# Two rows of their own for a token's two expert products, and scatters that skip empty slots

## The chip, the core and the metric

The kernel runs on one core of one Trainium2 chip. Time is device microseconds of one execution of the whole program. TensorE (PE) does the matmuls, VectorE (DVE), ScalarE (ACT) and GpSimd (POOL) the rest, SyncE (SP) issues loads. DMAs issued from SP and ACT and the indirect DMAs (a list of row numbers on chip says which rows of DRAM are read or written) issued from POOL move the data.

## The reference

Two layers of a diffusion network over 512 tokens of width 1024 (256 latent, 256 context). Layer 0 is neighbourhood attention and an mLSTM, then a mixture of experts; layer 1 is grouped-query attention, then a mixture of experts over the latent tokens. What is touched is the mixture of layer 0:

```python
def moe(h, router_w, router_b, w1, w3, w2):
    ...                                  # sigmoid scores, the best group of 4 experts,
    _, local = lax.top_k(sel_in, TOP_K)  # its two best experts
    e_idx = g_idx[:, None] * EXP_PER_GROUP + local
    w = jnp.take_along_axis(scores, e_idx, axis=-1)
    w = w / w.sum(axis=-1, keepdims=True)
    ...
    for e in range(N_EXPERTS):
        y = y + comb[:, e:e + 1] * ((jax.nn.silu(h @ w1[e]) * (h @ w3[e])) @ w2[e])
```

16 experts, 512 tokens, two experts for each: 1,024 products of a token and an expert, each a row of 1024 numbers, and each token's result is the sum of its two.

## The kernel before

Everything is float32. Weights come in pieces of 1 MB (`wtile`, L132, `w`) by SP into a ring of slots; for most matmuls each piece is split by ACT (`hi`, L286) and DVE (`lo`, L287) into two halves of the precision, and PE does three products instead of one.

**The first expert stage** (`moe_rows`, L509 onwards) lies at about 412 to 660 us. The router gives each product a place in a list of its expert (`pos`) and a weight (`wts`). Products are worked in 12 blocks of 128 slots: nine blocks hold one expert, three ("small", blocks 2, 5, 8, 11) hold two experts of 64 slots each. Experts 0 and 1 are fixed as blocks 0 and 1; the others are sorted by their counts into places (`lpos`, `lwts`). So 1,536 slots take 1,024 products. For block i:

- `table(i)` (L632) makes, from a one-hot matrix `oh` and matmuls into a PSUM tile `ad`, the list of row numbers `idx` (L612), the weights `we` (L613) and, in small blocks, a second list `idx2` (L640) for the upper 64 slots. Each list has six buffers. An empty slot gets the number 512 + slot (`home`, `pcol`). It then issues on POOL `gather` (L625): 128 rows of `rows` in DRAM go to `xg`. `table(i)` is written four blocks ahead of its use (`LEAD`).
- `x_turn`, `up`, `gated`, `a_turn`, `down_` transpose the rows and do the two projections up, the product, and the projection down.
- In `down_` the rows are multiplied with `we` into `ys`, and `scatter` (L630) adds them into `yacc` in DRAM, by an indirect DMA that accumulates. Small blocks do this in two halves of 64 rows, one made by ACT (L759) and one by DVE (L760). Blocks 10 and 11 (`DIR`) are not scattered; matmuls put them back on chip at the end (`put_back`, L909).

At the end, `yacc` is read back by two DMAs of 1 MB (L889) into slots of the weight ring, added to `put_back`'s sums by matmuls with an identity (`sums`, L915), and the residual is formed on DVE (`residual0`, L774).

**The clearing.** Adding needs zeros: `clear` (L1569) fills with zeros the rows 512 to 639 of `rows` and all 640 rows of `yacc`, by six DMAs of 512 KB on ACT's queue. It is called in the middle of layer 0's attention, about 218 to 229 us. Near it stand attention's exponentials on ACT (L1466) and the copies of projected values `mo` out of the PSUM tile `pj` (L1562); PE transposes into `pj` (L208) and runs the projection L1358 between pieces of attention.

**What sets the order.** Instructions stand on each engine in the order that a scheduler gives them at build time from the order of the code and its own estimates of durations; each engine runs its list in order. A buffer that is used again makes its writer wait for the last reader. Each DMA of SP and ACT signals one of eight semaphores (DMAHW0 to 7) in turn, and waits until the last DMA on its semaphore has landed; POOL's do the same with eight others (DMASW0 to 7).

Of the kernel before, what the change touches and what calls it, by code (L numbers as in the profile page):

```python
# [16 lines left out]
P = 128  # L17
# [66 lines left out]
def _model(tc, nc, ctx, A, out, dbg):  # L84
# [80 lines left out]
    for b in range(NB):  # L165
        V.tensor_scalar(pcol[:, b:b + 1], pidx, float(b * P - T), None, op0=OP.add)
    home = const.tile([P, 1], F32, name="home")
    V.tensor_scalar(home, pidx, float(T), None, op0=OP.add)
    sl = const.tile([P, J, 32], F32, name="sl")
# [155 lines left out]
    def moe_front(l, lat0, A2, pool):  # L325
# [36 lines left out]
        def finish(rt, put_row, brow, lgb, counts=None):  # L362
# [63 lines left out]
            rows_half(1)  # L426
            return pos, wts, msk

# [90 lines left out]
    def moe_rows(finish, shift, rows, yacc, fst, st, rt, ahead1, stream):  # L519
# [24 lines left out]

        pos, wts, msk = finish(rt, put_row, *shift, counts)
        bg(99)
# [9 lines left out]
        lpos, lwts = rt.tile([P, nb, NE], F32, name="lpos"), rt.tile([P, nb, NE], F32, name="lwts")  # L556
        GP.memset(aux[:, :, :, 3].bitcast(F32), 0.0)

# [64 lines left out]
        def gather(idx, tag="xg"):  # L623
            xg = wt_([P, D], tag)
            GP.indirect_dma_start(out=xg, out_offset=None, in_=rows[:, :],  # L625
                                  in_offset=bass.IndirectOffsetOnAxis(ap=idx[:, :1], axis=0))
            return xg

        def scatter(ys, idx):
            GP.indirect_dma_start(out=yacc[:, :], out_offset=bass.IndirectOffsetOnAxis(ap=idx[:, :1], axis=0),  # L630
                                  in_=ys, in_offset=None, compute_op=OP.add)

        def table(i):
            l, m = BLOCKS[i][0], len(BLOCKS[i])
            IDX[i], WE[i] = wt_([P, 1], "idx", I32), wt_([P, 1], "we")
            oh = one_hot(i)
            tb = slot_rows(oh, lambda b: aux[:, b, l:l + m, :], IDX[i], WE[i], m)
            if m == 2:
                IDX2[i] = wt_([HALF, 1], "idx2", I32)
                V.tensor_tensor(IDX2[i], tb[HALF:, 4:5], home[HALF:], op=OP.add)  # L640
            if i:
                XG[i] = gather(IDX[i])
            return oh
# [86 lines left out]
        def down_(i):  # L730
# [18 lines left out]
            if i in DIR:  # L749
                Y[i] = wt_([P, D], "ys" if i < DIR[-1] else "xh", F32R), wt_([P, D], "xg", F32R)  # L750
                for c in range(2):
                    yh, yl = (y[:, c * 512:(c + 1) * 512] for y in Y[i])
                    SC.activation(yh, yp[c], AF.Copy, scale=WE[i])
                    V.scalar_tensor_tensor(yl, yp[c], WE[i], yh.bitcast(F32), op0=OP.mult, op1=OP.subtract)
            elif is_small(i):
                ys = [wt_([P, D], "ys")[0:HALF] for _ in range(2)]
                for c in range(2):
                    s = slice(c * 512, (c + 1) * 512)
                    SC.activation(ys[0][:, s], yp[c][0:HALF], AF.Copy, scale=WE[i][0:HALF])  # L759
                    V.tensor_tensor(ys[1][:, s], yp[c][HALF:], WE[i][HALF:, 0:1].to_broadcast([HALF, 512]), op=OP.mult)  # L760

                scatter(ys[0], IDX[i][0:HALF])
                scatter(ys[1], IDX2[i])
            else:
                ys = wt_([P, D], "ys")
                for c in range(2):
                    SC.activation(ys[:, c * 512:(c + 1) * 512], yp[c], AF.Copy, scale=WE[i])
                scatter(ys, IDX[i])
            yield
# [18 lines left out]

        for dst, src in ((lpos, pos), (lwts, wts)):
            for b in range(0, nb, 2):  # L790
# [71 lines left out]
        with tc.issue_after(turned0.ins):  # L862
            put_aux(aux[:, :, FIX:], lpos[:, :, FIX:], lwts[:, :, FIX:])

# [8 lines left out]
        for i in range(n_ + 1):  # L873
# [9 lines left out]
            if i == n_:  # L883
                while stream.todo:
                    stream.load()
                ahead1(AH1)
                yr = [wslot().rearrange("p (a c) -> p a c", a=2) for _ in range(2)]
                for b in range(2):
                    pin(SY.dma_start(yr[b], yacc[b * 2 * P:(b + 1) * 2 * P, :].rearrange("(a p) c -> p a c", p=P)))  # L889
                ahead1(6)  # L890
# [41 lines left out]
    def moe_chip(finish, shift, fst, rt, rowp):  # L932
# [20 lines left out]

        pos, wts, msk = finish(rt, put_row, *shift, counts)
        fst.close()
# [609 lines left out]

    rows = dram.tile([T + P, D], F32, name="rows")
    yacc = dram.tile([T + P, D], F32, name="yacc")

    def clear(dep):  # L1569

        V.tensor_scalar(jp, ones, dep, 0.0, op0=OP.mult, op1=OP.mult)
        z = jp[:, None, :].to_broadcast([P, J, P])
        SC.dma_start(rows[T:, :].rearrange("p (a c) -> p a c", a=J), z)
        for b in range(NB + 1):
            SC.dma_start(yacc[b * P:(b + 1) * P, :].rearrange("p (a c) -> p a c", a=J), z)
# [452 lines left out]
```

## Time and profile before

| | |
|---|---|
| time, three runs | 1099.27, 1099.69, 1100.06 us (median 1099.69) |
| profiled execution | 1100.19 us, span 1098.3 us |
| mean granted TensorE clock | 0.958 of full speed |
| PE busy | 984.2 us (90% of the span) |
| DVE, ACT, POOL busy | 559.7, 399.6, 91.1 us |
| weight queue q1 | 290.23 MB, 66.8% of the span of 16 DMA engines |
| gathers and scatters, q0 | 11.01 MB, 3.8% |
| queue q10, with the clearing | 3.47 MB, 1.1% |
| indirect DMAs of the first expert stage | 11 gathers, 13 scatters |

The span runs from the first instruction to the last, and the time includes what lies around it. The share of busy time is a mean over stages with different limits, so the rows further down are of single stretches. A DMA share of 1 says that all 16 DMA engines had work the whole time. "Idle before, <- X" says for how long the engine had stood still ahead of an instruction, and what it waited for last.

### The profile page before, as it was taken

How to read it: one execution, taken by the hardware profiler on the slowest of the kernel's cores; microseconds unless marked ns; L12 is line 12 of the kernel's file. 1: busy time of each engine (PE TensorE's matmuls, PEld its weight loads, DVE VectorE, ACT ScalarE, POOL GpSimd, SP SyncE). 2: the span in 40 equal slices, each digit the busy share in tenths (PEclk: the TensorE clock that was granted, in tenths of full speed). 3: DMA queues.
4: the chain of work that ended last, by engine and by line, in shares of the span. 5: the costliest groups of instructions: out<-in, count | busy, mean ns of one | idle time of the engine just before them, and what ended most of it. 6: DMA issues, size and time to landing. Idle time of an engine off the chain costs nothing.

```text
span 1098.3 us, 14558 instructions
## 1 busy us (share of the span) xinstructions
PE 984.2 (90%) x5327; PEld 616.7 (56%) x5327; DVE 559.7 (51%) x1333; ACT 399.6 (36%) x735; POOL 91.1 (8%) x87
## 2 busy tenths in 40 slices
PE   5799999999999559999899999799998899988865
PEld 1577845556776357565566545468766454433322
DVE  3543389645877659575465623745766621101101
ACT  2532254437445227464535533324344121111100
POOL 0300000002000301211120100410100100000000
PEclk9899999999999769999989999899999799999988
DMA  9932237492328519999999999560198599999993
GB/s 376 300 123 83 77 146 256 168 340 77 123 109 322 215 56 361 388 392 395 401 404 383 409 401 371 201 232 2 61 357 348 205 419 420 420 419 420 421 419 113
DMA packets 71580, 305.70 MB, mean 278 GB/s; under 512 B 6096, under 2 KB 27856, under 8 KB 41168
## 3 DMA queue, kind: packets, MB, share of 16 engines
q1 hardware_dynamic: 61904, 290.23, 66.8%
q0 software_dynamic: 3072, 11.01, 3.8%
q10 hardware_dynamic: 6528, 3.47, 1.1%
q8 instruction: 44, 0.72, 0.3%
q14 instruction: 32, 0.26, 0.1%
HBM read 293.16 MB, written 11.53 MB: 277 GB/s over the span
## 4 chain that ended last, share of the span: by engine, by line
PE 30%; DMA 14%; DVE 4%; ACT 1%; issue 1%; POOL 0%; SPq 0%; DVEq 0%; ACTq 0%; POOLq 0%
DMA w<-in_exp_w_dram 13%; PE o L1011 5%; PE pj L1358 4%; PE o L235 3%; PE o L1050 2%; PE o L1886 1%; PE t L1358 1%; PE pj L998 1%; PE a L1871 1%; PE a L261 1%; PE o L1358 1%; DVE lo L287 1%; DMA xg<-rows,idx 1%; PE ad L261 1%; PE t L1882 1%; PE t L681 1%
## 5 line engine op out<-in xcount | busy, mean ns | idle before, releaser
L287 DVE TENSOR_TENSOR lo<-w,hi 128x1024 fp32r<-128x1024 f32 (+2 forms) x170 | 179.6, 1077 | 52.2 <-ACT hi L286 45.7
L286 ACT CAST hi<-w 128x1024 fp32r<-128x1024 f32 (+2 forms) x172 | 156.7, 928 | 111.0 <-PE o L1358 37.8
L1011 PE MATMUL o<-w,x 128*64 128x512 f32 x280 | 67.8, 596 | 0.0
L1028 DVE TENSOR_TENSOR ac<-ac,o 64x512 f32<-64x512 f32 x13 | 9.0, 691 | 110.5 <-ACT ac L1027 110.5
L702 PE MATMUL o<-lo,xh 128*128 128x512 f32 x128 | 51.8, 404 | 6.8 <-DVE lo L287 6.8
L681 PE MATMUL o<-w,xh 128*64 128x512 f32 x128 | 56.2, 595 | 0.1
L683 PE MATMUL o<-w,xh 128*64 128x512 f32 x128 | 56.2, 594 | 0.0
L261 PE MATMUL ad<-w,sl 128*32 128x512 f32 x320 | 50.8, 614 | 3.2 <-DMA w<-in_ada_w_dram 3.1
L701 PE MATMUL o<-hi,xh 128*128 128x512 f32 x128 | 51.6, 403 | 2.2 <-ACT hi L286 1.7
L703 PE MATMUL o<-hi,xl 128*128 128x512 f32 x128 | 50.9, 398 | 0.9 <-DVE xl L652 0.9
L1358 PE MATMUL pj<-h_hi,hi 128*128 128x512 f32 x104 | 43.8, 421 | 5.0 <-ACT h_hi L1345 2.6
L1027 ACT ACTIVATE ac<-o 64x512 f32<-64x512 f32 x13 | 7.7, 590 | 107.9 <-PE o L1011 63.2
L1358 PE MATMUL pj<-h_hi,lo 128*128 128x512 f32 x104 | 43.4, 418 | 0.2 <-DVE lo L287 0.2
L1358 PE MATMUL pj<-h_lo,hi 128*128 128x512 f32 x104 | 43.4, 417 | 0.0
L1011 PEld LDWEIGHTS o<-w,x 128*64 128x64 f32 x280 | 20.6, 137 | 37.9 <-issue 36.6
L235 PE MATMUL o<-w,x 128*32 128x512 f32 x256 | 31.4, 637 | 7.6 <-DMA w<-in_exp_w_dram 7.6
L681 PEld LDWEIGHTS o<-w,xh 128*64 128x64 f32 x128 | 17.0, 137 | 34.6 <-issue 33.4
L710 DVE TENSOR_TENSOR ac<-ac,o 128x512 f32<-128x512 f32 x12 | 8.2, 684 | 49.7 <-PE o L683 46.1
L1050 PE MATMUL o<-w,at 128*64 128x512 f32 x120 | 33.0, 597 | 0.0
L702 PEld LDWEIGHTS o<-lo,xh 128*128 128x128 f32 x128 | 24.6, 192 | 14.5 <-DVE lo L287 9.7
L1081 DVE SCALAR_TENSOR_TENSOR yl<-o,we,yh 128x512 fp32r<-128x512 f32 x12 | 8.9, 750 | 40.9 <-ACT yh L1080 40.9
L701 PEld LDWEIGHTS o<-hi,xh 128*128 128x128 f32 x128 | 24.5, 191 | 9.3 <-ACT hi L286 3.5
(589 smaller groups left out, 2269.4 us busy)
## 6 DMA issues: line engine op xcount, KB each, us to landing
w<-in_exp_w_dram SPq DMA_DIRECT2D x190, 1024.0 KB, 18.4
w<-in_ada_w_dram SPq DMA_DIRECT2D x48, 1024.0 KB, 6.7
w<-in_even_w_in_dram SPq DMA_DIRECT2D x12, 1024.0 KB, 12.1
w<-in_odd_w_in_dram SPq DMA_DIRECT2D x6, 1024.0 KB, 12.6
XT<-in_xT_dram SPq DMA_DIRECT2D x2, 2048.0 KB, 8.3
w<-in_even_w_out_dram SPq DMA_DIRECT2D x4, 1024.0 KB, 7.8
w<-in_odd_w_out_dram SPq DMA_DIRECT2D x4, 1024.0 KB, 9.0
yacc<-jp ACTq DMA_DIRECT2D x5, 512.0 KB, 9.7
```

The source lines that it names most:

```text
L235: done = PE.matmul(out[32 * q:32 * q + 32, :], lhsT=lhsT, rhs=rhs, start=start, stop=stop)
L261: PE.matmul(ps[32 * q:32 * q + 32, :], lhsT=sl[:, k, :], rhs=w[:, 0, q * 512:(q + 1) * 512], start=(k == 0), stop=(k == J - 1))
L286: SC.copy(hi, w)
L287: eng.tensor_tensor(lo, w, hi.bitcast(F32), op=OP.subtract)
L681: with_last = PE.matmul(out[HALF:], lhsT=lhsT[:, HALF:], rhs=rhs[1], start=start, stop=stop)
L683: PE.matmul(out[0:HALF], lhsT=lhsT[:, 0:HALF], rhs=rhs[0], start=start, stop=stop)
L701: PE.matmul(h_, lhsT=XH[i][:, k, :], rhs=hi[:, k % 2, :], start=(k == 0), stop=False)
L702: PE.matmul(h_, lhsT=XH[i][:, k, :], rhs=lo[:, k % 2, :], start=False, stop=False)
L703: PE.matmul(h_, lhsT=XL[i][:, k, :], rhs=hi[:, k % 2, :], start=False, stop=(k == J - 1))
L1011: PE.matmul(h[64 * c:64 * c + 64, :], lhsT=x[:, k, :], rhs=ws[c][:, i, :], start=(k == 0), stop=(k == J - 1))
L1050: PE.matmul(y[c][64 * i:64 * i + 64, :], lhsT=a[:, k, :], rhs=row_of(ws[q, i], k % 2)[:, c * 512:(c + 1) * 512], start=(k == 0), stop=(k = ...
L1358: f = (lambda a, b, **k: PE.matmul(ps, lhsT=b, rhs=a, **k)) if flip else (lambda a, b, **k: PE.matmul(ps, lhsT=a, rhs=b, **k))
```

## The change

In words: every token has two rows in `yacc`, row t for its first and row 512 + t for its second product, so that no two products meet and nothing has to be added in DRAM. The router's rank of a product among its token's two (0 or 1, `rank`) travels with `pos` (coded as rank * 1024 + pos through the sorting, decoded behind it) into the fourth column of `aux`, and from there into `idx2`, which every scattered block now has. Scatters are plain writes; an empty slot's number is 1,024 or more, and a bounds check skips it, in gathers too. A small block makes one `ys` of 128 rows (both halves by ACT) and one scatter: ten scatters instead of 13. `yacc` has 1,024 rows: eight clearing DMAs of 512 KB instead of five, and none for `rows` any more, so eight in place of six. Four reads of 1 MB bring `yacc` back, and four additions on DVE join the second half to the first ahead of `sums`.

```diff
-        V.tensor_scalar(pcol[:, b:b + 1], pidx, float(b * P - T), None, op0=OP.add)
+        V.tensor_scalar(pcol[:, b:b + 1], pidx, float(b * P - 2 * T), None, op0=OP.add)
...
-    V.tensor_scalar(home, pidx, float(T), None, op0=OP.add)
+    V.tensor_scalar(home, pidx, float(2 * T), None, op0=OP.add)
...
         put_aux(aux[:, :, 0:FIX], pos[:, :, 0:FIX], wts[:, :, 0:FIX])
+        V.tensor_scalar(aux[:, :, 0:FIX, 3], turn_[:, :, 0:FIX], float(T), None, op0=OP.mult)
...
             GP.indirect_dma_start(out=xg, out_offset=None, in_=rows[:, :],
-                                  in_offset=bass.IndirectOffsetOnAxis(ap=idx[:, :1], axis=0))
+                                  in_offset=bass.IndirectOffsetOnAxis(ap=idx[:, :1], axis=0), bounds_check=T - 1, oob_is_err=False)
...
             GP.indirect_dma_start(out=yacc[:, :], out_offset=bass.IndirectOffsetOnAxis(ap=idx[:, :1], axis=0),
-                                  in_=ys, in_offset=None, compute_op=OP.add)
+                                  in_=ys, in_offset=None, bounds_check=2 * T - 1, oob_is_err=False)
...
-            if m == 2:
-                IDX2[i] = wt_([HALF, 1], "idx2", I32)
-                V.tensor_tensor(IDX2[i], tb[HALF:, 4:5], home[HALF:], op=OP.add)
+            if i not in DIR:
+                IDX2[i] = wt_([P, 1], "idx2", I32)
+                for k in range(m):
+                    s = slice(P // m * k, P // m * (k + 1))
+                    V.tensor_tensor(IDX2[i][s], tb[s, 4 * k + 3:4 * k + 4], IDX[i][s], op=OP.add)
...
-            elif is_small(i):
-                ys = [wt_([P, D], "ys")[0:HALF] for _ in range(2)]
...
-                    SC.activation(ys[0][:, s], yp[c][0:HALF], AF.Copy, scale=WE[i][0:HALF])
-                    V.tensor_tensor(ys[1][:, s], yp[c][HALF:], WE[i][HALF:, 0:1].to_broadcast([HALF, 512]), op=OP.mult)
-
-                scatter(ys[0], IDX[i][0:HALF])
-                scatter(ys[1], IDX2[i])
             else:
...
-                scatter(ys, IDX[i])
+                scatter(ys, IDX2[i])
...
+        V.scalar_tensor_tensor(code, turn_, 1024.0, pos, op0=OP.mult, op1=OP.add)
+        for dst, src in ((lpos, code), (lwts, wts)):
...
+            V.tensor_scalar(second, lp, 1024.0, float(T), op0=OP.is_ge, op1=OP.mult)
+            V.scalar_tensor_tensor(lp, second.bitcast(F32), -1024.0 / T, lp, op0=OP.mult, op1=OP.add)
...
-                yr = [wslot().rearrange("p (a c) -> p a c", a=2) for _ in range(2)]
-                for b in range(2):
+                yr = [wslot().rearrange("p (a c) -> p a c", a=2) for _ in range(4)]
+                for b in (0, 2, 1, 3):
                     pin(SY.dma_start(yr[b], yacc[b * 2 * P:(b + 1) * 2 * P, :].rearrange("(a p) c -> p a c", p=P)))
...
+        for b in range(2):
+            for a in range(2):
+                V.tensor_tensor(yr[b][:, a], yr[b][:, a], yr[2 + b][:, a], op=OP.add)
...
-        SC.dma_start(rows[T:, :].rearrange("p (a c) -> p a c", a=J), z)
-        for b in range(NB + 1):
+        for b in range(2 * NB):
             SC.dma_start(yacc[b * P:(b + 1) * P, :].rearrange("p (a c) -> p a c", a=J), z)
```

Three places where the order of instructions moves. First, DVE in the middle of the expert stage, where the table of block 11 is made (`idx_4964` of before and `idx_5014` of after are its list, in two halves; `idx_4776` that of block 10; `oh` a one-hot matrix, `al` and `ys` belong to earlier blocks). Before:

```order
L612 TENSOR_SCALAR idx_4776<-ad_4780,home_88 128x1 [waits DMASW7_49,DMASW4_49,PE_49]
L613 TENSOR_REDUCE we_4777<-ad_4780 128x1
L601 TENSOR_TENSOR oh_5535<-slots_75,lpos_3301 128x512
L726 TENSOR_TENSOR al_4761<-pj_4755,ah_4760 128x512 [waits Activation_49]
L601 TENSOR_TENSOR oh_5543<-slots_75,lpos_3301 128x512 [waits PE_49]
L612 TENSOR_SCALAR idx_4964<-ad_4968,home_88 64x1 [waits DMASW0_49,DVE_49]
L612 TENSOR_SCALAR idx_4964<-ad_4968,home_88 64x1
L760 TENSOR_TENSOR ys_4769<-t_4730,we_3917 64x512 [waits DMASW3_49,Activation_49]
L287 TENSOR_TENSOR lo_4803<-w_4800,hi_4802 128x1024 [waits DMAHW2_49,Activation_49]
L760 TENSOR_TENSOR ys_4769<-t_4731,we_3917 64x512 [waits Activation_49]
```

After:

```order
L612 TENSOR_SCALAR idx_4822<-ad_4826,home_88 128x1 [waits PE_49]
L613 TENSOR_REDUCE we_4823<-ad_4826 128x1
L601 TENSOR_TENSOR oh_5587<-slots_75,lpos_3303 128x512
L728 TENSOR_TENSOR al_4809<-pj_4803,ah_4808 128x512 [waits Activation_49]
L612 TENSOR_SCALAR idx_5014<-ad_5018,home_88 64x1 [waits DMASW6_49,PE_49]
L612 TENSOR_SCALAR idx_5014<-ad_5018,home_88 64x1
L601 TENSOR_TENSOR oh_5595<-slots_75,lpos_3303 128x512
L287 TENSOR_TENSOR lo_4851<-w_4848,hi_4850 128x1024 [waits DMAHW4_49,Activation_49]
L613 TENSOR_REDUCE we_5015<-ad_5018 64x1 [waits Activation_49]
```

The list of block 11 waited for DMASW0, the semaphore on which the gather of block 10 signals; now it waits for DMASW6, that of the gather of block 5 (and for PE's `ad`). The two products `ys` of a small block on DVE are gone.

Second, ACT in attention, where the clearing stands (`pT`, `oa` and `p` belong to attention). Before:

```order
L1573 DMA rows<-jp 1024x1x128 [waits DMAHW3_49]
L1575 DMA yacc<-jp 1024x1x128 [waits DMAHW4_49]
L1475 COPY pT<-t 128x4x128 [waits PE_49]
L1575 DMA yacc<-jp 1024x1x128 [waits DMAHW6_49]
L1575 DMA yacc<-jp 1024x1x128 [waits DMAHW7_49]
L1486 CAST oa<-o 128x256 [waits PE_49]
L1575 DMA yacc<-jp 1024x1x128 [waits DMAHW1_49]
L1575 DMA yacc<-jp 1024x1x128 [waits DMAHW2_49]
L1562 COPY mo<-pj 128x512
L1466 ACTIVATE p,sm<-a,mx,rq 128x256 [waits DVE_49,Activation_49] x2
```

After:

```order
L1575 DMA yacc<-jp 1024x1x128 [waits DMAHW3_49]
L1575 DMA yacc<-jp 1024x1x128 [waits DMAHW4_49]
L1476 COPY pT<-t 128x4x128 [waits PE_49]
L1575 DMA yacc<-jp 1024x1x128 [waits DMAHW6_49]
L1575 DMA yacc<-jp 1024x1x128 [waits DMAHW7_49]
L1487 CAST oa<-o 128x256 [waits PE_49]
L1575 DMA yacc<-jp 1024x1x128 [waits DMAHW1_49]
L1575 DMA yacc<-jp 1024x1x128 [waits DMAHW2_49]
L1575 DMA yacc<-jp 1024x1x128 [waits DMAHW4_49]
L1575 DMA yacc<-jp 1024x1x128 [waits DMAHW5_49]
L1563 COPY mo<-pj 128x512
L1467 ACTIVATE p,sm<-a,mx,rq 128x256 [waits DVE_49,Activation_49] x2
```

The six clears are followed by two more ahead of the copy of `mo`. The last one uses DMAHW5; the last DMA on that semaphore is a load of `even_w_out` that SP issues between the second and the third clear.

Third, PE just behind that place (`ad` is a projection of the conditioning, `y` its result, `p` attention's probabilities, `oa`, `ka`, `qz` attention's operands). Before:

```order
L1483 MATMUL o<-pT,va 64x256 x7
L261 MATMUL ad<-w,sl 32x512 x16
L208 MATMUL pj<-ident,y 128x128 x4
L1453 MATMUL a<-ka,qz 128x256
L1358 MATMUL pj<-h_hi_253,hi 128x512
L1358 MATMUL pj<-h_hi_253,lo 128x512
L1358 MATMUL pj<-h_lo_261,hi 128x512
```

After:

```order
L1484 MATMUL o<-pT,va 64x256 x7
L261 MATMUL ad<-w,sl 32x512 x16
L208 MATMUL pj<-ident,y 128x128 x4
L1475 MATMUL t<-ident,p 128x128 x2
L1454 MATMUL a<-ka,qz 128x256
L1359 MATMUL pj<-h_hi_253,hi 128x512
L1359 MATMUL pj<-h_hi_253,lo 128x512
```

Two transposes of `p` have moved up behind the transpose into `pj`, ahead of the projection (L1358, now L1359); before, they stood behind the projection's 24 matmuls.

## Rows read from the trace of the kernel before

**Rows 1.** Stretches: busy of PE, PEld, DVE, ACT, POOL; clock, DMA share, GB/s.

```profile
540.00:580.00 40.00, 33.40 (x148) 20.77 (x148) 19.87 (x25) 16.54 (x20) 7.00 (x5) 0.91 1.02 400
580.00:620.00 40.00, 36.59 (x165) 21.58 (x162) 23.18 (x25) 22.68 (x28) 3.26 (x2) 1.00 1.02 406
420.00:650.00 230.00, 217.60 (x1020) 137.09 (x1020) 134.79 (x161) 116.42 (x144) 30.66 (x21) 0.99 1.02 395
```

**Rows 2.** Chain of waits: start us, us, what; first and last of four.

```profile
555.82 24.18 DMA w<-in_exp_w_dram
...
624.36 23.32 DMA w<-in_exp_w_dram
```

**Rows 3.** DMA in 412:660: packets, MB, share; issues: count, KB, us to landing.

```profile
q1 hardware_dynamic: 11908, 86.71, 84.4%
...
q0 software_dynamic: 2946, 10.52, 16.4%
...
w<-yacc SPq DMA_DIRECT2D x2, 1024.0 KB, 19.5
```

**Rows 4.** PE in time: start us, us, what, [idle before <- releaser].

```profile
545.18 0.49 PE L701 MATMUL o<-hi,xh 128*128 128x512 f32 x1 [0.86 <-ACT hi L286]
...
551.42 0.79 PE L702 MATMUL o<-lo,xh 128*128 128x512 f32 x1 [5.74 <-DVE lo L287]
```

**Rows 5.** POOL and DVE in time around 540, same columns.

```profile
539.97 1.26 POOL L625 DMA_INDIRECT xg<-rows,idx  x1 [13.66 <-DVE we L613]
...
548.88 0.45 DVE L612 TENSOR_SCALAR idx<-ad,home 64x1 int32<-64x1 f32 x2 [7.32 <-DMA xg<-rows,idx]
```

**Rows 6.** Table by stretch, behind the hole and after it.

```profile
548.80:555.60 6.80, 4.18 (x10) 3.31 (x11) 6.55 (x9) 1.04 (x1) 2.40 (x2) 0.50 1.01 420
556.00:560.00 4.00, 4.00 (x19) 3.31 (x18) 2.52 (x3) 2.13 (x3) 0.00 (x0) 1.00 1.05 364
```

**Rows 7.** Waits of PE, in 580:620 and in 620:660: us in total, times, longest.

```profile
PE o L702 <- DVE lo L287: 1.1, 2, 0.8
...
PE t L746 <- DVE lo L287: 0.5, 1, 0.5
```

**Rows 8.** ACT and its DMA issues in time around the clearing.

```profile
227.19 1.50 ACTq L1575 DMA_DIRECT2D yacc<-jp  x2
228.73 0.59 ACT L1562 COPY mo<-pj 128x512 f32<-128x512 f32 x1 [1.18 <-issue]
229.21 0.57 ACT L1466 ACTIVATE p<-a,mx,rq 128x256 f32<-128x256 f32 x1
```

**Rows 9.** DMA issues in 224.0:224.4: count, KB, us to landing.

```profile
w<-in_even_w_out_dram SPq DMA_DIRECT2D x1, 1024.0 KB, 8.4
```

**Rows 10.** PE and DVE in time at the same place.

```profile
230.65 0.66 PE L208 MATMUL pj<-ident,y 128*128 128x128 f32 x4
...
231.74 0.48 PE L1358 MATMUL pj<-h_hi,hi 128*128 128x512 f32 x1
...
231.51 0.34 DVE L1471 TENSOR_SCALAR p<-p,sm 128x256 f32<-128x256 f32 x1
```

**Rows 11.** Table by stretch, 200 to 260.

```profile
200.00:230.00 30.00, 29.84 (x170) 15.76 (x172) 16.78 (x56) 11.50 (x34) 0.00 (x0) 1.00 0.69 239
230.00:260.00 30.00, 30.00 (x140) 19.20 (x133) 16.40 (x51) 14.79 (x37) 4.66 (x3) 1.00 0.61 228
```

**Rows 12.** One of the page's groups (busy, mean ns); DVE in time, 556.

```profile
L287 DVE TENSOR_TENSOR lo<-w,hi 128x1024 fp32r<-128x1024 f32 (+2 forms) x170 | 179.6, 1077 | 52.2 <-ACT hi L286 45.7
...
556.00 0.16 DVE L640 TENSOR_TENSOR idx<-ad,home 64x1 int32<-64x1 f32 x1
```

**Rows 13.** DVE in time at the end of the stage.

```profile
668.95 1.61 DVE L754 SCALAR_TENSOR_TENSOR xg<-t,we,xh 128x512 fp32r<-128x512 f32 x2 [8.47 <-ACT xh L753]
...
673.40 1.77 DVE L774 SCALAR_TENSOR_TENSOR XT<-a,mod,XT 128x256 f32<-128x256 f32 x4 [2.83 <-PE a L915]
...
681.79 0.87 DVE L774 SCALAR_TENSOR_TENSOR XT<-t,mod,XT 128x256 f32<-128x256 f32 x2 [2.91 <-PE t L915]
```

More of the change, by code (lines that the diff above doesn't have):

```diff
@@ L426, in finish @@
             rows_half(1)
-            return pos, wts, msk
+            return pos, wts, rank
         return step, finish
@@ L543, in counts @@
                 PE.matmul(cn, lhsT=ones, rhs=msk[:, b, :], start=(b == 0), stop=(b == nb - 1))
-        pos, wts, msk = finish(rt, put_row, *shift, counts)
+        pos, wts, turn_ = finish(rt, put_row, *shift, counts)
         bg(99)
@@ L556, in moe_rows @@
         lpos, lwts = rt.tile([P, nb, NE], F32, name="lpos"), rt.tile([P, nb, NE], F32, name="lwts")
-        GP.memset(aux[:, :, :, 3].bitcast(F32), 0.0)
         def put_aux(aux, pos, wts):
@@ L754, in down_ @@
                     V.scalar_tensor_tensor(yl, yp[c], WE[i], yh.bitcast(F32), op0=OP.mult, op1=OP.subtract)
-            elif is_small(i):
-                ys = [wt_([P, D], "ys")[0:HALF] for _ in range(2)]
-                for c in range(2):
-                    s = slice(c * 512, (c + 1) * 512)
-                    SC.activation(ys[0][:, s], yp[c][0:HALF], AF.Copy, scale=WE[i][0:HALF])
-                    V.tensor_tensor(ys[1][:, s], yp[c][HALF:], WE[i][HALF:, 0:1].to_broadcast([HALF, 512]), op=OP.mult)
-                scatter(ys[0], IDX[i][0:HALF])
-                scatter(ys[1], IDX2[i])
             else:
@@ L787, in moe_rows @@
         lst = blocks_beyond(rt, cn, cap, CAP, n, y, ctl)
-        for dst, src in ((lpos, pos), (lwts, wts)):
+        code = y[:, 2 * DYN * DYN:][:, 0:nb * NE].rearrange("p (b e) -> p b e", b=nb)
+        V.scalar_tensor_tensor(code, turn_, 1024.0, pos, op0=OP.mult, op1=OP.add)
+        for dst, src in ((lpos, code), (lwts, wts)):
             for b in range(0, nb, 2):
@@ L862, in moe_rows @@
         with tc.issue_after(turned0.ins):
-            put_aux(aux[:, :, FIX:], lpos[:, :, FIX:], lwts[:, :, FIX:])
+            lp, second = lpos[:, :, FIX:], aux[:, :, FIX:, 3]
+            V.tensor_scalar(second, lp, 1024.0, float(T), op0=OP.is_ge, op1=OP.mult)
+            V.scalar_tensor_tensor(lp, second.bitcast(F32), -1024.0 / T, lp, op0=OP.mult, op1=OP.add)
+            put_aux(aux[:, :, FIX:], lp, lwts[:, :, FIX:])
             second = aux[:, :, FIX + BIG:, 0].rearrange("p b (i l) -> p b i l", l=2)[:, :, :, 1]
@@ L952, in counts @@
                 PE.matmul(cn, lhsT=ones, rhs=msk[:, b, :], start=(b == 0), stop=(b == nb - 1))
-        pos, wts, msk = finish(rt, put_row, *shift, counts)
+        pos, wts, _ = finish(rt, put_row, *shift, counts)
         fst.close()
@@ L1563, in mlstm_proj @@
                 yield
-    rows = dram.tile([T + P, D], F32, name="rows")
-    yacc = dram.tile([T + P, D], F32, name="yacc")
+    rows = dram.tile([T, D], F32, name="rows")
+    yacc = dram.tile([2 * T, D], F32, name="yacc")
     def clear(dep):
```

## The prediction

> **What bounds the kernel now.** I read the first expert stage (about 412 to 660 us) before the rest, because the diff changes its gathers and scatters, and in it the table of stretches first. Both resources are full at once: over 420 to 650 PE is busy 217.60 of 230.00 us and the DMA share is 1.02 [rows 1]. So PE has only 12.4 us to give back in this stage, whatever happens to the transfers. From 540 on, PE shows holes: 6.6 us in 540:580 and 3.4 us in 580:620 [rows 1]. Next the chain of waits: from 555.82 to about 648 it consists of weight loads that take 21 to 24 us each to land, four in a row [rows 2]. There the transfers pace the kernel, and PE only just keeps up with them. Third the DMA queues in the stage: the weight queue q1 moves 86.71 MB in 84.4% of 248 us, 2.41 us per MB; the gather and scatter queue q0 moves 10.52 MB in 16.4%, 40.7 us, 3.87 us per MB [rows 3]. The bytes of gathers and scatters cost 1.6 times those of the weights.
>
> **Part 1, the wait at the table of block 11: -7.7 us.** PE stands still 5.74 us before 551.42 for a low half of weights from DVE [rows 4]. DVE had been stopped 7.32 us, until 548.88, in front of an `idx` write, by the landing of a gather that POOL issued at 539.97 [rows 5]. The order shows why: `idx` has six buffers, and table 11 takes the buffer of table 10, which is free only when the gather that reads it has landed. In the changed kernel scatters read `idx2` instead, the `idx` buffers come free at the gathers, and table 11 waits for a semaphore of a gather issued many blocks earlier. The gather on which DVE stood is no longer in its way: -5.74 us. The stall also dropped the granted clock: 548.8 to 555.6 ran at 0.50 of full speed [rows 6], the 1.2 GHz level. The ten matmuls there took 4.18 us, 0.42 each, against 0.21 at full clock from 556 on (4.00 us for 19) [rows 6]: 2.0 us. With the hole gone I take this as gone too. What is late next at that place are the weight loads, part 2.
>
> **Part 2, fewer and cheaper packets: -4.0 us (0 to -4.8).** 1,024 products stand in 1,536 slots, so about a third of the rows that are gathered or scattered is skipped. At q1's 2.41 us per MB the 10.52 MB would take 25.4 us; the other 15.3 us I put to the accumulating scatters, the only thing on q0 that is not a plain copy. After: two thirds of 10.52 MB at 2.41 is 16.9 us, 23.8 us less DMA work in the stage. Against it stands 2 MB more read back from `yacc`, 5 us at the same price. PE can use only its holes: 3.4 us in 580:620, most of it waits for the halves that ACT and DVE make out of a load that has just landed [rows 7], and of the same kind 0.9 us at 545 [rows 4] and 0.5 us near 653 [rows 7]: 4.8 in all. I take 4.0, since loads and PE stay close together. The lower end is 0: a skipped row may cost what a copied one does, and no row here shows a skip or a plain scatter. Merging the two half scatters of a small block into one, and moving two products from DVE to ACT there, I cost at nothing: they stand behind the weights' halves, with DVE busy 134.79 and ACT 116.42 of 230 us [rows 1].
>
> **Part 3, the clearing: +5.6 us (0 to +8).** This is the part that speaks against the change. Before, six DMAs on ACT's queue write zeros; after, eight, and the two new ones stand ahead of the copy of `mo` out of the PSUM tile `pj`. Issuing two took 1.50 us and the copy began right behind them, at 228.73 [rows 8]. But each issue first waits for a semaphore, and the order shows that the last new one waits for that of a load of `even_w_out`, issued at 224.26, which took 8.4 us to land [rows 9]: 232.7. Then comes 0.75 us of issue (half of 1.50), so the copy starts at about 233.5 instead of 228.73. Behind it on ACT stand the exponentials of attention, behind those DVE's scaling, and on PE a transpose into `pj` which began at 230.65 [rows 10]. It will wait until 234.1. The order now puts two transposes of `p` right after it, which need those exponentials (two of 0.57 each [rows 8], so 235.1) and DVE's reciprocal and scaling (the latter 0.34 [rows 10], together 0.5): 235.6, then about 0.8 us of PE work before the projection, which began at 231.74 [rows 10]. It begins at about 236.4, 4.6 us later. PE is busy 30.00 of 30 us in 230:260 [rows 11], so no idle time there takes this up. The clock falls after a hole: I add 1.0 us, half of what the longer one cost at 551. Two more clears are also 1 MB more for the DMA, which has room (share 0.69 and 0.61 [rows 11]).
> First the row, then the rule: two issues took 1.50 us on ACT [rows 8]. The Trainium skill, "DMA: Bandwidth & Descriptors", section "Issuing engines are not separate DMA queues", says that an issuing engine's queue decides only about the sequencer time of starting a DMA, small beside the DMA itself. By that price the clears would cost ACT 1.5 us and the forecast would be 5 us lower. The wait that the order shows ahead of the issue is why I don't take it.
>
> **Part 4, routing and tables: +0.5 us (0.3 to 1.0).** Two or three more DVE instructions of 128x56 to 128x64 elements or less lie on the serial routing chain before the stage; the nearest row is a small `idx` instruction of 0.16 us [rows 12]. The `idx2` of later tables lies beside other work.
>
> **Part 5, the sums at the end: +0.5 us (-0.5 to +5).** Four adds of 128x1024 go to DVE behind the last products of block 11; that shape, as a split of weights, takes 1.08 us on average, 4.3 to 4.8 us for four [rows 12]. Before, DVE finished these products at 670.56, idled 2.83 us, did residuals from 673.40, and idled 2.91 us again before 681.79 [rows 13]. The adds fill 670.56 to 675.3; 16 residuals of 0.44 us then end at 682.4 to 683.5, against 683.56 before. So the adds lie in idle time, provided the rows of `yacc` are there. Two reads landed 19.5 us after issue [rows 3]; two more at 2.5 us each come 5 us later, and the DMA work saved in front of them is larger.
>
> **Sum.** -7.7 - 4.0 + 5.6 + 0.5 + 0.5 = -5.1 us. The profiled execution took 1100.19 us (span 1098.3), 0.5 us above the median of 1099.69: 1095.1 against its own time, **1094.6** against the median.
>
> **Rivals.**
> A, the clearing costs only its issue: the load lands earlier or ACT has slack. For it: the copy had 1.9 us of slack before PE's transpose, and rows 8 show no wait of this kind. Against it: the order's wait. Without the 5.6 us: 1089.0. The Trainium skill's rule named in part 3 ("DMA: Bandwidth & Descriptors") would give this case.
> B, the weights land no sooner for PE: only part 1 is gained. For it: weight landings stay at 2.4 us per MB and PE was full until 540, so relief may come where it isn't needed. -7.7 + 6.6 = -1.1: 1098.6, no change that can be measured.
> C, slower: skipped slots and plain writes cost the DMA as much as before. Then the chain of loads from 555 to 648 stays where it is, and the stall removed in part 1 only lets PE arrive earlier at the same loads; the gain is 0 to 2, the clears and the rest stay, 6.6: 1104 to 1106. It decides when the stage gains less than 4.4 us. For it: the chain is all DMA there; against it: 3.87 against 2.41 us per MB, of which the accumulate is the only difference in kind.
>
> **How the numbers follow.** Forecast 0.50, A 0.15, B 0.17, C 0.18. A measurement of this kernel can tell about 0.2%, 2.2 us: faster is below 1097.5, slower above 1101.9. Forecast, with bounds of parts 2, 3 and 5, lies in 1090 to 1099, mostly faster (0.46 of 0.50). Faster 0.46 + 0.15 = 0.61, same 0.17 + 0.04 = 0.21, slower 0.18. The range 1088 to 1103 leaves out the lower end of A and most of C, under 2 in 10.
>
> **What would show it.** Part 1: no DVE wait of microseconds at an `idx` line near 540, granted clock 1.00 there. Part 2: q0 under 20 us in the stage, and PE's holes between 580 and 620 gone. Part 3: a pause on ACT from 229 to about 233 and a PE hole of 3 to 5 us at 231, with a low clock behind it. Part 5: residuals ending about 13 us behind block 11's last product, as now. It would be wrong if the transfers of q0 don't shrink (C), or if ACT runs on at 229 (A).

## The result and the profile after

| | before | after |
|---|---|---|
| median | 1099.69 us | 1105.78 us |
| runs | 1099.27 to 1101.36 | 1104.15 to 1106.74 |
| profiled execution, span | 1100.19, 1098.3 us | 1106.74, 1104.9 us |
| mean granted clock | 0.958 | 0.953 |
| q0 in the stage, a window of 262 us | 11.01 MB, 16.1%, 42.2 us | 7.43 MB, 7.7%, 20.2 us |

The time is 1.0052 times that of before, 95% interval 1.0027 to 1.0077: slower by 0.5%, about 6 us, and not faster by 5. To see where, I take the same PE instruction in both traces and subtract its start of before from that of after. The changed kernel is later by:

| place in the kernel before | later by | step since the line above |
|---|---|---|
| up to 229 us | 0.6 us | |
| 292 to 398 us, behind the attention with the clears | 14.8 | +14.2 |
| 423 us, behind the routing | 15.2 | +0.4 |
| 545 us, just ahead of the stall of [rows 4] | 14.9 | -0.3 |
| 557 us, just behind it | 8.25 | -6.7 |
| 654 us, end of the weights of the stage | 7.4 | -0.9 |
| 706 us on to the last matmul | 7.5 | +0.1 |

So one place costs 14 us, one gives 7, and the rest is small. The stage with the cheaper transfers gives hardly more than its one stall.

**The place that costs.** ACT in time in the changed kernel, where the kernel before had [rows 8] (columns: start us, us, what, idle before and what ended it):

```profile
227.78 15.46 ACTq L1575 DMA_DIRECT2D yacc<-jp  x4
243.27 0.58 ACT L1563 COPY mo<-pj 128x512 f32<-128x512 f32 x1 [15.13 <-issue]
```

The copy of `mo` stood at 228.73 before; it now stands at 243.27, and what held it 15.13 us is not a wait for a semaphore but the issue of DMAs. The line of the clears by itself, first in the kernel before, then in the one after (times of one issue in ns: least, median, longest; first and last start):

```profile
L1575 ACTq DMA_DIRECT2D yacc<-jp x5: 520/679/939, 218.7 to 227.7; - x5
```

```profile
L1575 ACTq DMA_DIRECT2D yacc<-jp x8: 521/684/9005, 218.7 to 238.3; - x8
...
  ACT mo L1563: 15.1, 1
...
DMA to landing us min/median/max: 3.6/10.4/18.5
```

The seventh issue ran from 229.30 to 238.30, the eighth 4.9 us, to 243.23. The load of `even_w_out` whose semaphore the eighth had to wait for landed at 233.43, well before that one began. The trace holds every packet of ACT's queue q10 (for a clear 1,024 of 512 bytes, here called pieces, and 16 of 4 bytes), so one can count how many of them were issued and not yet done when an issue began:

| clear | packets not yet done as its issue began | its issue took |
|---|---|---|
| before, fifth of six | 570 | 0.52 us |
| before, sixth | 1,521 | 0.94 us |
| after, sixth of eight | 1,528 | 0.92 us |
| after, seventh | 2,423 | 9.00 us |
| after, eighth | 2,009 | 4.89 us |

When the two long issues ended, 2,014 and 2,517 packets were not yet done. PE in time, where [rows 10] stood before, and DVE's reciprocal ahead of the scaling:

```profile
243.91 1.12 PE L208 MATMUL pj<-ident,y 128*128 128x128 f32 x4 [12.61 <-ACT mo L1563]
...
246.10 0.99 PE L1359 MATMUL pj<-h_hi,hi 128*128 128x512 f32 x1
```

```profile
244.45 0.16 DVE L1471 RECIPROCAL sm<-sm 128x1 f32<-128x1 f32 x1 [15.85 <-ACT p L1467]
```

PE stands still for 12.61 us, from 231.30 on, and the table by stretch (busy of PE, PEld, DVE, ACT, POOL, then clock, DMA share, GB/s) shows the clock that follows:

```profile
230.00:260.00 30.00, 17.27 (x76) 11.32 (x65) 8.77 (x26) 7.05 (x18) 0.00 (x0) 0.77 0.67 238
235.70:249.40 13.70, 5.37 (x15) 4.19 (x16) 3.67 (x12) 3.28 (x8) 0.00 (x0) 0.50 0.90 324
```

Against 30.00 of 30 us busy before [rows 11], PE has 17.27. From 235.7 to 249.4 the clock is at 0.50, the 1.2 GHz level.

**The stage.** Table 11 no longer waits, and the two stretches of [rows 1], moved by 15 us, are fuller: 38.17 for 33.40, and 37.08 for 36.59.

```profile
555.81 0.44 DVE L612 TENSOR_SCALAR idx<-ad,home 64x1 int32<-64x1 f32 x2
```

```profile
555.00:595.00 40.00, 38.17 (x177) 21.49 (x175) 19.48 (x24) 18.88 (x24) 4.45 (x4) 1.00 1.01 418
595.00:635.00 40.00, 37.08 (x165) 25.00 (x165) 26.38 (x27) 25.33 (x31) 2.21 (x2) 1.00 1.01 418
```

The DMA queues, as in [rows 3] but over 262 us, which hold the whole stage (packets, MB, share of 16 engines; for the weight loads count, KB, median us to landing); the kernel before first, from 398 to 660, then the one after, from 413 to 675:

```profile
q1 hardware_dynamic: 12052, 87.76, 81.1%
q0 software_dynamic: 3072, 11.01, 16.1%
...
w<-in_exp_w_dram SPq DMA_DIRECT2D x84, 1024.0 KB, 21.8
```

```profile
q1 hardware_dynamic: 14191, 93.30, 87.5%
q0 software_dynamic: 3024, 7.43, 7.7%
...
w<-in_exp_w_dram SPq DMA_DIRECT2D x84, 1024.0 KB, 18.3
```

The transfers did become about as cheap as forecast: 20.2 us for 42.2, and the weight loads land 18.3 us behind their issue at the median, 21.8 before. But PE's waits in 595:635 (us in all, times, longest) are the ones that stood there before [rows 7]:

```profile
PE o L703 <- ACT hi L286: 0.9, 1, 0.9
PE pj L721 <- DVE ac L712: 0.8, 1, 0.8
PE o L704 <- DVE lo L287: 0.8, 1, 0.8
PE t L748 <- DVE lo L287: 0.5, 1, 0.5
```

They are no waits for a load. The cast `hi` of L703, and with it `lo` of L704, is of a piece that had landed at 616.19, 6.7 us before the cast; `ac` of L712 had itself waited for PE; and the piece of the `lo` ahead of L748 had landed at 589.42, 4.8 us before it. ACT in time ahead of the same wait for `hi` one block earlier, where [rows 4] stood, first before, then after:

```profile
543.51 0.68 ACT L759 ACTIVATE ys<-t,we 64x512 f32<-64x512 f32 x1 [3.79 <-PE t L683]
```

```profile
558.44 0.69 ACT L760 ACTIVATE ys<-t,we 128x512 f32<-128x512 f32 x1 [3.79 <-PE t L685]
559.02 1.03 ACT L286 CAST hi<-w 128x1024 fp32r<-128x1024 f32 x1
```

The cast that PE wants stands on ACT behind an eviction of `ys` (a product scaled on its way out of PSUM), and that waits for PE's own product `t`; the piece to be cast had landed at 549.64, 9.4 us earlier. It is a matter of order on ACT, and the kernel before has the same 3.79 us there and the same 0.86 us on PE behind it [rows 4]. An earlier landing would not have filled these holes.

### The profile page after: what moved, and what is told of

Its sections match the earlier page's. It is cut to its first block, busy times and chain, and to the rows that moved or that the text cites. A ratio compares the mean times of both kernels' runs of the same rounds, so it can differ in the third digit from the quotient of the medians.

```text
span 1104.9 us, 14598 instructions
## 1 busy us (share of the span) xinstructions
PE 983.5 (89%) x5327; PEld 617.6 (56%) x5327; DVE 560.3 (51%) x1344; ACT 398.5 (36%) x735; POOL 81.9 (7%) x83
## 3 DMA queue, kind: packets, MB, share of 16 engines
q0 software_dynamic: 3024, 7.43, 1.8%
## 4 chain that ended last, share of the span: by engine, by line
PE 50%; DMA 5%; DVE 5%; ACT 2%; issue 1%; POOL 0%; ACTq 0%; DVEq 0%; SPq 0%; POOLq 0%
PE o L683 5%; DMA w<-in_exp_w_dram 5%; PE o L1012 5%; PE pj L1359 4%; PE o L235 3%; PE o L704 3%; PE o L705 2%; PE o L703 2%; PE t L683 2%; PE o L1051 2%; DVE lo L287 2%; PE pj L999 1%; PE o L1886 1%; PE t L748 1%; PE t L749 1%; PE t L1359 1%
## 5 line engine op out<-in xcount | busy, mean ns | idle before, releaser
L703 PE MATMUL o<-hi,xh 128*128 128x512 f32 x128 | 50.9, 397 | 2.2 <-ACT hi L286 1.7
L704 PE MATMUL o<-lo,xh 128*128 128x512 f32 x128 | 51.2, 400 | 1.6 <-DVE lo L287 1.5
L1359 PE MATMUL pj<-h_hi,hi 128*128 128x512 f32 x104 | 44.8, 431 | 5.0 <-ACT h_hi L1346 2.6
L1359 PE MATMUL pj<-h_lo,hi 128*128 128x512 f32 x104 | 44.0, 423 | 0.0
L1359 PE MATMUL pj<-h_hi,lo 128*128 128x512 f32 x104 | 43.8, 421 | 0.2 <-DVE lo L287 0.2
L712 DVE TENSOR_TENSOR ac<-ac,o 128x512 f32<-128x512 f32 x12 | 8.2, 682 | 49.6 <-PE o L685 46.0
L704 PEld LDWEIGHTS o<-lo,xh 128*128 128x128 f32 x128 | 24.0, 188 | 9.7 <-DVE lo L287 5.1
L703 PEld LDWEIGHTS o<-hi,xh 128*128 128x128 f32 x128 | 24.1, 188 | 9.2 <-ACT hi L286 3.5
```

The lines of the kernel that those rows point to most:

```text
L703: PE.matmul(h_, lhsT=XH[i][:, k, :], rhs=hi[:, k % 2, :], start=(k == 0), stop=False)
L704: PE.matmul(h_, lhsT=XH[i][:, k, :], rhs=lo[:, k % 2, :], start=False, stop=False)
L1359: f = (lambda a, b, **k: PE.matmul(ps, lhsT=b, rhs=a, **k)) if flip else (lambda a, b, **k: PE.matmul(ps, lhsT=a, rhs=b, **k))
```

## The experiments

The expectations put two theories of the clears against each other. **Q**: issuing itself is what holds ACT; the queue takes no more pieces until earlier ones have drained (a clear of 512 KB in rows of 512 bytes is 1,024 pieces). **S**: the semaphore that an issue first waits for, as the prediction had it. For the stage, **L**: the list of block 11 alone is worth its stall; **W**: behind the stall the weight loads are next late, so cheaper transfers are needed too. **T** is what came of that: the two are worth something only together. Ratios are to executions of the kernel before that ran beside each experiment (medians 1100.07 to 1100.84 us), with 95% intervals.

**Two clears issued by POOL** (changed kernel):

```diff
-            SC.dma_start(yacc[b * P:(b + 1) * P, :]...
+            (SC if b < 6 else GP).dma_start(yacc[b * P:(b + 1) * P, :]...
```

> The changed kernel, with its last two clearing DMAs issued by POOL instead of ACT; all else as it is. Theory Q (ACT is held while it issues, because its queue of small pieces is full: 9.0 and 4.9 us for the seventh and eighth clear): ACT runs on at 229 us, PE has no hole there, and the 15 us of shift go: about 1091 us. Rival S (the wait for the landed load that the prediction priced, some 5 us, and the rest of the shift from the other order around it): about 1100 us.

1103.23 us, 1.0032 (1.0016 to 1.0048). ACT in time, and the clears' line:

```profile
227.24 11.02 ACTq L1575 DMA_DIRECT2D yacc<-jp  x2
238.30 0.59 ACT L1563 COPY mo<-pj 128x512 f32<-128x512 f32 x1 [10.70 <-issue]
```

```profile
L1575 ACTq DMA_DIRECT2D yacc<-jp x6: 520/894/9887, 218.1 to 228.4; - x6
L1575 POOL DMA_DIRECT2D yacc<-jp x2: 1018/1055/1092, 217.7 to 218.7; - x2
```

The forecast of 1091 from Q missed, and S's 1100 too. ACT issues only six clears, as before the change, and still the last takes 9.89 us; the load on its semaphore had landed at 218.89, so it is no wait of S's kind. What differs is that POOL issued its 1 MB from 217.7 on, beside ACT's first clears (in the trace 288 packets on q0). ACT's queue drained more slowly: 2,702 of its packets were done at 228.37, for 3,672 at 228.34 in the changed kernel. So its sixth clear began with 2,498 packets not yet done, about as many as the seventh had found in the changed kernel. It isn't only how many DMAs ACT issues, but how full its queue is when it issues.

**The kernel before with two more clears**, nothing else:

```diff
-    yacc = dram.tile([T + P, D], F32, name="yacc")
+    yacc = dram.tile([T + 3 * P, D], F32, name="yacc")
...
-        for b in range(NB + 1):
+        for b in range(NB + 3):
```

> The kernel before, with two more clearing DMAs of 512 KB on ACT's queue (two more blocks of rows in DRAM that nothing reads); nothing else. Theory Q: the same hole as in the changed kernel, 12 to 13 us of PE idle at 231 us and a low clock behind it: 1099.7 + 15 = about 1114 us. Rival S: 1104 to 1106 us.

1113.33 us, 1.0125 (1.0101 to 1.0148); ACT in time:

```profile
227.49 15.26 ACTq L1575 DMA_DIRECT2D yacc<-jp  x4
242.79 0.58 ACT L1562 COPY mo<-pj 128x512 f32<-128x512 f32 x1 [14.94 <-issue]
```

The two clears alone cost 13.6 us, and PE is later by 14.6 to 15.1 us behind them, 0.3 of it from before them. That is the whole of the +14.2 in the table of places, and nothing else of the change is needed for it. Q's number was right, S's (1104 to 1106) was not.

**Clears half as fine**, the same eight, with rows of 1,024 bytes from a tile of zeros twice as wide:

```diff
-        z = jp[:, None, :].to_broadcast([P, J, P])
+        z = zw[:, None, :].to_broadcast([P, NB, 2 * P])
...
-            SC.dma_start(yacc[...].rearrange("p (a c) -> p a c", a=J), z)
+            SC.dma_start(yacc[...].rearrange("p (a c) -> p a c", a=NB), z)
```

(`zw` is the wider tile; so that it finds room, `jp` and `maskb` share one tile, here and in the versions built on this one.)

> The changed kernel, with the zeros written in pieces of 1,024 bytes instead of 512 (a zero tile of 256 numbers a partition): the same eight DMAs of 512 KB at the same places with the same waits, half as many pieces. Theory Q (ACT is held because its queue of pieces is full): only the wait of the eighth clear for a landed load is left, ACT's copy starts near 234 us and PE's hole is 3 to 5 us: 1096 to 1097 us. Rival B (the bytes of the clears decide, not the pieces): the hole stays 12 us and the time about 1105 us.

1098.08 us, 0.9981 (0.9964 to 0.9998): 7.7 us better than the changed kernel, with the same DMAs, bytes and semaphores. ACT in time, the clears' line, and PE behind it:

```profile
230.13 6.80 ACTq L1575 DMA_DIRECT2D yacc<-zw  x4
236.98 0.59 ACT L1563 COPY mo<-pj 128x512 f32<-128x512 f32 x1 [6.48 <-DMA yacc<-zw]
```

```profile
L1575 ACTq DMA_DIRECT2D yacc<-zw x8: 521/621/1557, 221.1 to 236.4; - x8
```

```profile
237.62 1.11 PE L207 MATMUL pj<-ident,y 128*128 128x128 f32 x4 [3.96 <-ACT mo L1563]
```

No issue takes over 1.56 us any more, and none began with more than 1,056 packets not yet done. What is left is a wait for a landing, with a PE hole of 3.96 us. The row names a clear as what ended it, but the profile only infers that: the seventh clear's issue ends at 232.94, and the eighth's starts at 236.41, 0.02 us behind the landing of the `even_w_out` load on its semaphore (issued at 227.21, 9.2 us to landing). This is the wait that the prediction saw, at about its price: a hole of 3 to 5 us, and +5.6 us in all, where PE is set back here by 6.0 us, and by 4.5 and 4.8 in the two versions below with the same clears. S is real; it was hidden under Q.

**Four clears of 1 MB**, in rows of 1,024 bytes, so that no issue waits for the load either:

```diff
-        z = zw[:, None, :].to_broadcast([P, NB, 2 * P])
-        for b in range(2 * NB):
-            SC.dma_start(yacc[b * P:(b + 1) * P, :].rearrange("p (a c) -> p a c", a=NB), z)
+        z = zw[:, None, :].to_broadcast([P, 2 * NB, 2 * P])
+        for b in range(NB):
+            SC.dma_start(yacc[b * 2 * P:(b + 1) * 2 * P, :].rearrange("(p r) (a c) -> p (r a) c", p=P, a=NB), z)
```

> The same zeros of 1,024-byte pieces in four DMAs of 1 MB instead of eight of 512 KB, so that none of them is the one that waits for the landed load. Theory Q: fewer pieces in all than before (4,096 against 6,144) and no such wait: no hole on PE at 231 us, 1091 to 1092 us, which is faster than the kernel before. Rival B: 1105 us.

1092.63 us, 0.9937 (0.9913 to 0.9962): better than both kernels. ACT in time, and the stretch that had 17.27 us of PE:

```profile
226.61 1.25 ACTq L1575 DMA_DIRECT2D yacc<-zw  x2
227.91 0.58 ACT L1563 COPY mo<-pj 128x512 f32<-128x512 f32 x1 [0.93 <-issue]
```

```profile
230.00:260.00 30.00, 30.00 (x140) 19.89 (x137) 16.56 (x48) 13.84 (x35) 4.65 (x3) 1.00 0.69 264
```

PE is earlier than before by 1.7 us ahead of the stage and by 8.9 us at 652, so the stage gives 7.2 us.

**The clears in two groups**, four a step earlier, with the narrow rows:

```diff
-    def clear(dep):
+    def clear(dep, part):
...
-        for b in range(2 * NB):
+        for b in part:
...
-        if pr == CLR:
-            clear(oa_lo[pr][:, 0:1].bitcast(F32))
+        if pr in (CLR - 1, CLR):
+            clear(oa_lo[pr][:, 0:1].bitcast(F32), range(0, NB) if pr < CLR else range(NB, 2 * NB))
```

> The changed kernel, with its eight clearing DMAs in two groups of four on ACT's queue, the first group one step of attention earlier. Theory Q: the queue is never full, so no hole: about 1091 us, as with POOL issuing two. Rival S: each group still waits for loads that signal on the same semaphores, so part of the shift stays: 1095 to 1101 us.

1095.6 us, 0.9960 (0.9947 to 0.9973), where Q gave 1091 on the assumption that the queue would not fill at all. S's range of 1095 to 1101 holds the number, but not by S's waits: of the ACT issues, two still took 6.27 and 3.81 us, the loads on their semaphores had landed at 208.67 and 214.44, and the issues began with 2,062 and 2,223 packets not yet done:

```profile
220.92 6.27 ACTq L1575 DMA_DIRECT2D yacc<-jp  x1
...
227.26 3.81 ACTq L1575 DMA_DIRECT2D yacc<-jp  x1
```

Most of it now lies beside work of PE (holes of 1.50 and 0.44 us), and PE enters the stage 2.9 us late instead of 15. Moving the issues took most of the shift away here, but not all of it.

Over the eleven traces, the 66 clears on ACT's queue that began with at most 1,917 packets not yet done took at most 1.57 us to issue, and the eight that began with 2,009 to 2,498 took 2.09 to 9.89 us.

**The kernel before with twelve buffers for `idx`**, so that table 11 has no buffer to wait for, and all transfers as they were:

```diff
-... "idx": 6, "idx2": 6, "we": 6},
+... "idx": 12, "idx2": 6, "we": 6},
```

> The kernel before, with twelve buffers for the lists of row numbers instead of six; nothing else. It takes the wait of DVE for the gather away, and leaves the accumulating scatters and the empty slots as they are. Theory L (the stall of 5.7 us and its low clock are worth what they show, and cheaper transfers are not needed for it): 1092 to 1093 us. Rival W (PE would only arrive earlier at weights that have not landed, as long as the transfers cost what they do): 1098 to 1100 us.

1100.3 us, 1.0008 (0.9995 to 1.0020). The stall is gone and PE is 6.1 us earlier at 559, but then:

```profile
575.52 0.61 PE L681 MATMUL o<-w,xh 128*64 128x512 f32 x1 [3.20 <-DMA w<-in_exp_w_dram]
```

Of the 6.1 us, 1.7 are left at 580 and 0.1 at 620. PE now arrives early at loads that come no sooner (21.7 us to landing at the median, 21.8 before). L falls, W holds.

**Accumulating scatters in the version with wider clears**, empty slots still skipped:

```diff
         def scatter(ys, idx):
...
-                                  in_=ys, in_offset=None, bounds_check=2 * T - 1, oob_is_err=False)
+                                  in_=ys, in_offset=None, bounds_check=2 * T - 1, oob_is_err=False, compute_op=OP.add)
```

> The kernel with eight clears in 1,024-byte pieces, and its scatters accumulate again (into the same two rows of a token, empty slots still skipped). It asks what the accumulate costs. If the accumulating write is what made the old scatters dear: q0's time in the stage rises from about 19 to 28 us, and part of the stage's gain of 7.9 us goes back, 2 to 4 us. If the skipping of empty slots alone is enough: the same time as the kernel with the 1,024-byte clears, within 1 us.

1104.55 us, 1.0035 (1.0020 to 1.0049): 6.5 us more than the version with plain scatters (1098.08), where 2 to 4 were expected. q0 in 262 us, and PE:

```profile
q0 software_dynamic: 3024, 7.43, 11.5%
```

```profile
582.36 0.70 PE L682 MATMUL o<-w,xh 128*64 128x512 f32 x1 [3.81 <-DMA w<-in_exp_w_dram]
```

The same bytes take 30.1 us (11.5% of 262) with accumulation, 20.4 without (7.8%), and the weight loads land 22.2 us behind their issue, 19.0 without. PE is 5.8 us late at 524, 0.1 at 577, past the place where the stall had been, and 5.8 again at 602: what the list gives back is taken by the loads, as in the experiment before.

**Empty slots written to spare rows**, plain scatters that skip nothing, in the same version:

```diff
-                                  in_=ys, in_offset=None, bounds_check=2 * T - 1, oob_is_err=False)
+                                  in_=ys, in_offset=None)
...
-    yacc = dram.tile([2 * T, D], F32, name="yacc")
+    yacc = dram.tile([2 * T + P, D], F32, name="yacc")
```

> The kernel with eight clears in 1,024-byte pieces, and its scatters write the empty slots too, to spare rows (gathers still skip them, writes are plain). If the plain write is what counts: q0's time rises by 4 us only and the stage keeps its gain of 7.9 us, within 1 us. If the skipping counts: part of the gain, 2 us or more, goes back.

1098.1 us, 0.9980 (0.9967 to 0.9993), the same as with skipping. q0 has 9.02 MB and 9.0%, 23.6 us: skipping in the scatters saves about 3 us of DMA work and no time.

**The wait at table 11 put back, transfers cheap**: the version with four clears, with lists 10 and 11 in one buffer of their own:

```diff
-            IDX[i], WE[i] = wt_([P, 1], "idx", I32), wt_([P, 1], "we")
+            IDX[i], WE[i] = wt_([P, 1], "idxd" if i in DIR else "idx", I32), wt_([P, 1], "we")
```

> The fastest version so far (the changed kernel with four clears of 1 MB in 1,024-byte pieces), but with one buffer for the row lists of blocks 10 and 11, so that the list of block 11 waits for the gather of block 10 as in the kernel before. Cheap transfers with the stall; the kernel before with twelve list buffers was dear transfers without it. If the two are only worth something together (theory T): the stall of 5 to 6 us and its low clock come back, nothing behind makes up for them, and the time is 1099 to 1101 us, no gain over the kernel before. If cheap transfers are worth something by themselves (rival: loads land earlier and PE catches up behind the stall): 1093 to 1096 us.

1099.57 us, 1.0000 (0.9989 to 1.0012). DVE and PE in time:

```profile
548.74 0.45 DVE L611 TENSOR_SCALAR idxd<-ad,home 64x1 int32<-64x1 f32 x2 [7.52 <-DMA xg<-rows,idxd]
```

```profile
550.50 0.80 PE L703 MATMUL o<-lo,xh 128*128 128x512 f32 x1 [5.15 <-DVE lo L286]
```

The stall is there as in [rows 4, 5], and the gain is gone. With that the four cases are:

| | scatters accumulate | scatters plain |
|---|---|---|
| table 11 waits for gather 10 | 1099.69 (before) | 1099.57 |
| it doesn't | 1100.30 | 1092.63 |

The left column has the clears and the router of before, the right one four wide clears, which PE leaves 1.7 us earlier. Neither step alone brings anything that can be measured; together they bring 7 us. Undone one at a time in versions that are otherwise alike, each step costs nearly all of that: 6.5 us for the accumulation, 6.9 for the wait. T holds.

## Why the prediction was wrong

**Part 3 failed, in one step.** "Then comes 0.75 us of issue (half of 1.50)" took the price of an issue from a queue that still had room: the two issues behind the 1.50 us began with 570 and 1,521 packets not yet done. In the changed kernel the two new issues began with 2,423 and 2,009 and took 9.0 and 4.9 us. Everything behind it was followed correctly: ACT runs in order, so `mo`, the exponentials, DVE's reciprocal and PE's transposes all waited, and the projection began 14.4 us later (246.10 for 231.74), not 4.6. The step is +14.2 us in place of +5.6. The half clock behind it (13.7 us at 0.50, 5.37 us of them busy) is in that number. The wait for the semaphore of `even_w_out` was no error: with the pieces halved it stands alone, with a PE hole of 3.96 us. But it was only the second of two costs of the same instructions, and I stopped looking after the first.

The trace of the kernel before had the warning. On SP, the issues of `odd_w_in` loads (window 650 to 690; in 650 to 680, 4,962 of 6,029 packets were under 2 KB) took up to 9.06 us, with 3.09 at the median:

```profile
L132 SPq DMA_DIRECT2D w<-in_odd_w_in_dram x6: 378/3088/9062, 651.4 to 674.0; - x6
```

And the last clear's own issue already took 939 ns, for 520 to 690 before it.

In the prediction I set aside, because of the wait, the rule of the Trainium skill that the time an issuing engine's sequencer takes to start a DMA is usually small beside the DMA ("DMA: Bandwidth & Descriptors", section "Issuing engines are not separate DMA queues"). The trace differs from it here: the seventh clear's issue took 9.0 of the 18.5 us from its start to the clear's landing. The same section says that DMAs from different engines run on the same 16 DMA engines and interleave; the run with two clears on POOL agrees, where ACT's queue had 2,702 packets done at 228.4 us for 3,672 without POOL's.

**Part 1 was right in mechanism and nearly in size.** No wait at the `idx` line, clock 1.00 in 555:595, and 6.7 us gained between 545 and 557, for 7.7 forecast. But the sum booked it as a gain that stands by itself. The runs show that it doesn't: with accumulating scatters it is given back to the loads within 60 us (1100.3).

**Part 2 was right on the transfers and wrong on PE.** q0 fell to 20.2 us ("under 20" was the mark), and the accumulation had a large part in it, as argued: 9.7 us of DMA for the same bytes, where the prediction put 15.3 to the scatters before. But "most of it waits for the halves ... out of a load that has just landed" was wrong. Those holes, 0.5 to 0.9 us each, are still there, and where a cast or a split ends them, its load had landed 4.8 us or more earlier: what holds them open is the order on ACT and DVE, where work that waits for PE stands ahead. So the term was -0.9, not -4.0. The value of the cheap transfers lay elsewhere: they let part 1 be kept, which a sum of separate terms can't say.

**Part 4 was right, and part 5 nearly.** Routing cost 0.4 us (forecast 0.5). The adds take 4.62 us on DVE. Behind them the residuals end at 691.76, 15.5 us behind the start of block 11's last products, for 14.6 before: there, behind the last of [rows 13], stands one more row, which ends at 683.56. First that row, then the kernel after:

```profile
682.68 0.88 DVE L774 SCALAR_TENSOR_TENSOR XT<-a,mod,XT 128x256 f32<-128x256 f32 x2
```

```profile
676.25 1.61 DVE L756 SCALAR_TENSOR_TENSOR xg<-t,we,xh 128x512 fp32r<-128x512 f32 x2 [8.46 <-ACT xh L755]
677.78 4.62 DVE L904 TENSOR_TENSOR w<-w 128x1024 f32<-128x1024 f32 x4
685.40 1.66 DVE L767 SCALAR_TENSOR_TENSOR XT<-a,mod,XT 128x256 f32<-128x256 f32 x4 [3.00 <-PE a L916]
...
690.89 0.87 DVE L767 SCALAR_TENSOR_TENSOR XT<-a,mod,XT 128x256 f32<-128x256 f32 x2
```

So not all of the adds' time was idle before: DVE ends 0.9 us later, for 0.5 forecast. PE, at 706 us, shows 0.1 of it.

**The rivals.** C names the time that came, 1104 to 1106, but by a mechanism that did not happen: the transfers did get cheaper, and the stage gained 7.6 us, over C's point of 4.4. A, clears that cost only what their issue did before, is what the version with four clears does; its 1092.6 lies between A's 1089.0 and the forecast, mostly since part 2 gave 3 us less. B's "only part 1 is gained" is what the stage did, but not for B's reason: the loads did land sooner (18.3 us for 21.8), and where they did not, part 1's gain was lost again (1100.3). With the measured terms the sum closes: 0.6 + 14.2 + 0.4 - 0.3 - 6.7 - 0.9 + 0.1 = 7.4 us on PE (7.5 in the table, by rounding); the spans differ by 6.6 us, so about 0.9 us is given back outside the matmuls.

**Still open.** What sets the room of a queue was not measured apart. For the clears, the count of packets not yet done separates long issues from short ones (over 2,000, under 1,920), but one load of 1 MB on SP's queue in the changed kernel, at 357.48 us, took 2.1 us to issue with 288 packets not yet done, so the count is not the whole of it. The table of four cases mixes kernels that differ in more than its two steps; the two versions with one step undone do not.

## What to carry to other kernels

Price the issue of a DMA by the pieces that are already queued, not by the last quiet issue: on an engine that computes in order, a queue full of small pieces holds every instruction behind it, and wider pieces took most of that away here, and fewer DMAs with them the rest. A stall that is removed is worth its length only if what is next late there has slack; try the removal with and without the relief of the next resource before adding the two. Ahead of calling a short hole a wait for data, look at what its releaser was itself waiting for on its own engine.

## What the runs showed of the hardware that I had not expected

- One issue of a 512-KB DMA in 512-byte rows held ACT for up to 9.9 us; with 1,024-byte rows the longest was 1.57 us, and with four DMAs of 1 MB in such rows 0.70 us.
- The issue was long when about 2,000 packets or more of ACT's queue were issued and not yet done: 2.09 to 9.89 us from 2,009 to 2,498 packets, at most 1.57 us up to 1,917.
- Accumulating scatters took 9.7 us more of DMA time in the stage than plain ones of the same bytes (30.1 and 20.4 us, ten scatters and the gathers), and 6.5 us of the kernel's time.
- Leaving out the empty rows in plain scatters saved 1.59 MB and about 3 us of DMA time, and nothing of the kernel's time (1098.1 with, 1098.08 without them).
